# A decoder layer in split float32: weight halves of the memory stage split one unit ahead, squares summed from untransposed rows, output-stage splits at fixed pieces

## The chip, the core and the metric

One core of a Trainium2 chip runs the whole layer. The metric is the device time of one execution in microseconds (us), as the median over several.

## What is computed

One layer of a hybrid decoder for 512 tokens of width 2048, with 256 memory tokens of the same width, all in float32. What the change touches of it:

```python
mem_n = rms_norm(mem, norm_mem_g)
h = rms_norm(x, norm_in_g[layer])
proj = jnp.einsum('bsd,de->bse', h, w_in[layer])
...
mkv = jnp.einsum('bmd,de->bme', mem_n, w_mem_kv[layer])
mk, mv = jnp.split(mkv, 2, axis=-1)
...
merged = (g_a * jnp.einsum('bse,ed->bsd', ya, w_proj_a[layer])
          + g_b * jnp.einsum('bse,ed->bsd', yb, w_proj_b[layer])
          + g_m * jnp.einsum('bse,ed->bsd', ym, w_proj_m[layer]))
x = x + jnp.einsum('bsd,de->bse', merged, w_out[layer])
return rms_norm(x, norm_final_g)
```

`rms_norm` divides each token's row by the root of its mean square and multiplies by a gain. Between the projections and `merged` stand three attention branches, which the change leaves alone.

## The kernel before

**Arithmetic.** Every float32 operand of a large product is split in two parts, hi (the value rounded to TensorE's format, one ACT copy) and lo (value minus hi, one DVE subtraction), and a product is three matmuls: hi·hi, hi·lo, lo·hi. So each weight half of 128x1024 costs one SP transfer of 512 KB, one ACT and one DVE instruction (`load_half`, lines 85 to 92; `parts_1024`, 371 to 376). The split weights live in rings `whi` and `wlo` of three buffers each (WBUFS). `split` (160) does the same for activations.

**Buffers.** Tiles of 128x512 come from 25 buffers (`slot`), those of 128x1024 from 18 (`wide_tile`, shared with the raw weights), tiles of 128x256 from a ring of four (`half_tile`, 368). PSUM has four banks `acc` and four banks `att`.

**Order.** The program is written as one sequence. A planner of the framework orders the instructions of each engine from it: earlier lines have priority, but an instruction whose inputs or buffers are not free by the planner's own durations is passed by later ones. The result is a fixed order for each engine and DMA queue; on the chip each waits at its head.

**Stages.**
1. First projections (275 to 291): three units of w_in, each 2048 x 128, are multiplied by x transposed, in four groups of four k-tiles, while xT comes in. `Rows.cut` (207 to 226) scales and splits each k-tile of xT (216, 217), squares it on ACT (222) and adds the squares up on POOL (226). `Rows.scales` (228) sums over the partitions by one-column matmuls with ones (238), takes the reciprocal root and spreads it over a row (`hrow`) by diagonal matmuls.
2. Three more units of w_in (300 to 310, `project`, 114), 48 matmuls of 512 columns each. Beside them the memory tokens, transposed, are cut in the same way (thi, tlo), and xT is normalized in place (`normalize`, 294).
3. Memory keys (344 to 353): eight units of w_mem, 48 matmuls of 256 columns each. After a unit, DVE multiplies its result by `mrow` (350) and `forms(k)` (317) makes the sums and splits of a pair of k-tiles of h that the later seven-product scheme (Strassen-like, on 256-token halves) needs: four DVE sums, four splits, of which T12 and T3 go to wide tiles.
4. Memory values (354 to 359): two groups of four units, w_mem as the moving operand of 512 columns (`product_rows`, 120), two banks of 128 tokens each. A unit uses both its halves in each bank.
5. The attention branches and gates (to 1084), built on `Pair` (395): two units of w_in in seven products, a generator whose steps are interleaved with attention work. `begin` loads and starts the next pair. Each pair holds half tiles ha, hd and hb between its steps.
6. Output stage (1085 to 1141). The merged activations' parts were written to DRAM (`merged_forms`, 893) and are fetched again as `mg` tiles and split (`left`, `right`, `third_form`, 933 to 945, on `fetch_then`, 907, and `ahead_by`, 918, which fetches some jobs ahead of the split). There are two column pairs of 28 pieces; a piece is one w_out quarter or sum of quarters, split by `prepare` (994) up to two pieces ahead, and 12 matmuls of 512 columns. The seven forms of a pair, four pieces each, are B11, T1, T2, B21, T3, B22, T4, in this order. `multiply` (1006) pops one of the waiting jobs (`later`) after each piece: the right parts at pieces 0 to 7, the third forms at 8 to 15, the T4 parts at 16 to 23.
   After a form, DVE adds its bank to the residual tile (`add_block`, 1029). When a 128x512 block of the result is complete, `gained` (1036) squares it on ACT with a row sum, multiplies it by the final gain on POOL (1039) and, in the first column pair, stores it to DRAM (`rows_done`); the second pair fetches those back. `finish_row` (1043) applies the root of the row's mean square and writes the output. `gf`, the gain spread over the partitions, is loaded at the start of each column pair.

The projection and value loops before, in the lines that matter:

```python
    def project(src, act, tokens=S):
        cut = load_unit(src)
        ps = acc_bank()[:, :tokens]
        product(ps, cut, 0, act, NK)
        return ps
```

`load_unit` loads and splits a half when `product` first asks for it.

## Time and profile before

| | us |
|---|---|
| three timed runs | 2062.39, 2061.36, 2053.85 |
| median | 2061.36 |
| profiled execution | 2054.51 |
| its span, first to last instruction | 2052.7 |
| mean granted TensorE clock | 0.988 of full speed |

PE is TensorE, PEld its weight loads, DVE, ACT and POOL the vector, scalar and GpSimd engines, SP the queue that issues most loads. Times are counted from the start of the span. A wait is named by who waited, the instruction that released it, the us in total, how often and the longest. Matmuls overlap, so the time of one is longer than the step to the next.

### The profile page before, as it was taken

The page shows a single profiled execution, that of the slowest core. Times are in us where ns is not written, and L with a number is a line of the kernel's source. Part 1 is how long each engine was busy: PE and PEld are TensorE (multiplying, and loading weights), DVE is VectorE, ACT ScalarE, POOL GpSimd, SP SyncE. Part 2 cuts the span into 40 slices and gives each one's busy share as a digit, 9 for nine tenths or more (in the row PEclk, how much of TensorE's full clock was granted, in tenths as well). Part 3 has the DMA queues.
Part 4 walks back from the last instruction along what each step waited for, and adds up shares of the span by engine and source line. Part 5 has one row for each costly group of instructions (what it writes and reads, how often), then busy time and mean ns, then how long its engine had stood idle before and what let it go on. Part 6 is the DMA issues. An engine that isn't in the chain of part 4 may idle for free. (4 is left out here: it accounts for less than half of the span.)

```text
span 2052.7 us, 34930 instructions
## 1 busy us (share of the span) xinstructions
PE 1983.7 (97%) x14241; PEld 1870.4 (91%) x14241; DVE 1556.1 (76%) x1940; ACT 1018.8 (50%) x1572; POOL 199.2 (10%) x291
## 2 busy tenths in 40 slices
PE   8868999999999999999999999999999999999898
PEld 5767999889999999889999999998999999998676
DVE  7955777627888888527897979755888888888697
ACT  6624456424666655424646454554444444445445
POOL 4400011010000000001000000001000000012232
PEclk9989999999999999999999999999999999999999
DMA  8226344343332333433332332334434433447664
GB/s 286 88 95 200 129 135 144 129 142 108 98 98 95 101 99 124 149 118 104 103 99 94 104 97 89 114 134 160 157 137 156 138 128 123 156 146 275 213 201 163
DMA packets 88289, 278.52 MB, mean 136 GB/s; under 512 B 16480, under 2 KB 17504, under 8 KB 88128
## 3 DMA queue, kind: packets, MB, share of 16 engines
q1 hardware_dynamic: 70176, 218.72, 32.1%
q0 software_dynamic: 17808, 57.56, 8.2%
q8 instruction: 111, 1.82, 0.4%
q14 instruction: 50, 0.41, 0.1%
q10 hardware_dynamic: 144, 0.02, 0.0%
HBM read 244.76 MB, written 31.49 MB: 135 GB/s over the span
## 5 line engine op out<-in xcount | busy, mean ns | idle before, releaser
L374 ACT ACTIVATE whi<-raw 128x1024 fp32r<-128x1024 f32 x507 | 537.2, 1060 | 611.8 <-PE acc L385 376.9
L375 DVE TENSOR_TENSOR wlo<-raw,whi 128x1024 fp32r<-128x1024 f32 x507 | 622.8, 1229 | 178.3 <-ACT whi L374 167.9
L384 PE MATMUL acc<-kept,whi 128*128 128x256 f32 x2080 | 591.3, 284 | 6.0 <-DVE g L454 5.9
L386 PE MATMUL acc<-kept,wlo 128*128 128x256 f32 x2080 | 588.8, 283 | 0.0
L385 PE MATMUL acc<-kept,whi 128*128 128x256 f32 x2080 | 588.7, 283 | 0.0
L384 PE MATMUL acc<-T,whi 128*128 128x256 f32 x1560 | 442.2, 283 | 0.5 <-ACT ha L430 0.5
L385 PE MATMUL acc<-T,whi 128*128 128x256 f32 x1560 | 441.6, 283 | 0.0
L386 PE MATMUL acc<-T,wlo 128*128 128x256 f32 x1560 | 441.6, 283 | 0.0
L384 PEld LDWEIGHTS acc<-kept,whi 128*128 128x128 f32 x2080 | 399.0, 192 | 7.9 <-issue 7.1
L385 PEld LDWEIGHTS acc<-kept,whi 128*128 128x128 f32 x2080 | 399.1, 192 | 0.3
L386 PEld LDWEIGHTS acc<-kept,wlo 128*128 128x128 f32 x2080 | 399.0, 192 | 0.0
L384 PEld LDWEIGHTS acc<-T,whi 128*128 128x128 f32 x1560 | 299.3, 192 | 1.1 <-ACT ha L430 0.7
L385 PEld LDWEIGHTS acc<-T,whi 128*128 128x128 f32 x1560 | 299.4, 192 | 0.3
L386 PEld LDWEIGHTS acc<-T,wlo 128*128 128x128 f32 x1560 | 299.3, 192 | 0.0
L91 DVE TENSOR_TENSOR wlo<-raw,whi 128x1024 fp32r<-128x1024 f32 x78 | 95.7, 1236 | 149.5 <-ACT whi L90 149.5
L90 ACT ACTIVATE whi<-raw 128x1024 fp32r<-128x1024 f32 x78 | 81.6, 1056 | 167.7 <-PE acc L111 118.1
L110 PE MATMUL acc<-shi,whi 128*128 128x512 f32 x320 | 126.7, 396 | 0.5 <-ACT pr L137 0.5
L111 PE MATMUL acc<-slo,whi 128*128 128x512 f32 x320 | 126.8, 396 | 0.0
L112 PE MATMUL acc<-shi,wlo 128*128 128x512 f32 x320 | 126.0, 394 | 0.0
L423 DVE TENSOR_TENSOR raw<-raw 128x1024 f32<-128x1024 f32 x65 | 79.5, 1223 | 22.4 <-DMA raw<-in_w_in 20.7
L441 DVE TENSOR_TENSOR raw<-raw 128x1024 f32<-128x1024 f32 x65 | 79.4, 1221 | 0.9
L428 DVE TENSOR_TENSOR raw<-raw 128x1024 f32<-128x1024 f32 x65 | 79.3, 1221 | 0.9
(271 smaller groups left out, 2722.0 us busy)
## 6 DMA issues: line engine op xcount, KB each, us to landing
raw<-in_w_in SPq DMA_DIRECT2D x266, 512.0 KB, 3.7
raw<-in_w_out SPq DMA_DIRECT2D x48, 512.0 KB, 5.1
raw<-in_w_mem SPq DMA_DIRECT2D x32, 512.0 KB, 3.7
projected<-pr POOLq DMA_DIRECT2D x48, 256.0 KB, 2.6
pj<-projected POOLq DMA_DIRECT2D x48, 256.0 KB, 4.8
raw<-in_w_pm SPq DMA_DIRECT2D x16, 512.0 KB, 3.8
raw<-in_w_pa SPq DMA_DIRECT2D x16, 512.0 KB, 4.2
xraw<-in_xT SPq DMA_DIRECT2D x16, 256.0 KB, 5.4
```

What stands on the lines that cost most here:

```text
L90: nc.scalar.activation(hi, raw, AF.Copy)
L91: nc.vector.tensor_tensor(lo, raw, hi.bitcast(F32), op=OP.subtract)
L110: nc.tensor.matmul(ps, whi, hi[i], start=i == 0, stop=False)
L111: nc.tensor.matmul(ps, whi, lo[i], start=False, stop=False)
L112: nc.tensor.matmul(ps, wlo, hi[i], start=False, stop=i == n - 1)
L374: nc.scalar.activation(hi, raw, AF.Copy)
L375: nc.vector.tensor_tensor(lo, raw, hi.bitcast(F32), op=OP.subtract)
L384: nc.tensor.matmul(ps, hi[:, sl], f[0], start=start and k == 0, stop=False, skip_group_check=True)
L385: nc.tensor.matmul(ps, hi[:, sl], f[1], start=False, stop=False, skip_group_check=True)
L386: nc.tensor.matmul(ps, lo[:, sl], f[0], start=False, stop=stop and k == 7, skip_group_check=True)
L423: nc.vector.tensor_tensor(s, a21, a22, op=OP.add)
L441: nc.vector.tensor_tensor(s, s, a12, op=OP.add)
```

## The change

- `primed` loads a unit's weights and splits their first half. `project` and `product_rows` take a primed unit, split its second half, and prime the following unit (`follower`) once their matmuls are written, in one chain from the fourth w_in unit through the keys to the last value unit.
- In the memory keys `forms(m - 1)` comes ahead of the multiplication of unit m by mrow. The memory values stand after the definitions of the attention stage, and the first query pair is begun ahead of the last group's copies.
- `Rows.square` loads 128x1024 of x (eight times) or mem (four times) as they are, tokens on partitions, and ACT squares them in place with a sum per token; `scales` adds the two halves' sums on DVE. The transposed squares, the POOL additions and the one-column matmuls go.
- In the output stage a table `beside` says after which piece each split is made: right parts at 4 to 11, third forms two a piece at 12 to 15, T4 parts at 16 to 23, fetched three ahead. The `mg` tiles of 128x256 are half tiles. Squares go to an `att` bank. The gain multiplications move to DVE, after pieces 46 to 51; `rows_done` holds ungained blocks, `gf` is loaded and the blocks are fetched back ahead of B21 of the second column pair. `complete` is what is left of `gained`.

The diff, cut to its core (`M`, `held` and the rest are as before; `finish_row` names `gf[c // 2]` instead of `gf[1]`, and `mem` is a new argument):

```diff
@@ -111,26 +111,34 @@
-    def project(src, act, tokens=S):
+    def primed(src):
         cut = load_unit(src)
+        cut(0, P)
+        return cut
+
+    def project(cut, follower, act, tokens=S):
+
         ps = acc_bank()[:, :tokens]
+        cut(1024, P)
         product(ps, cut, 0, act, NK)
-        return ps
-
-    def product_rows(units, act, tiles, last=1):
+        return ps, primed(follower)
+
+    def product_rows(cut, units, act, tiles):
...
         banks = [acc_bank() for _ in tiles]
-        cuts = [load_unit(u) for u in units]
-        for group in [[u] for u in range(4 - last)] + [list(range(4 - last, 4))]:
+        for u in range(4):
+            now = cut
+            now(1024, P)
+            cut = primed(units[u]) if units[u] is not None else None
             for b, sl in zip(banks, tiles):
-                for k in [4 * u + kk for u in group for kk in range(4)]:
-                    whi, wlo = cuts[k // 4](k % 4 * 512, 512)
+                for k in range(4 * u, 4 * u + 4):
+                    whi, wlo = now(k % 4 * 512, 512)
                     nc.tensor.matmul(b, hi[k][:, sl], whi, start=k == 0, stop=False)
...
                     nc.tensor.matmul(b, lo[k][:, sl], whi, start=False, stop=k == NK - 1)
-        return banks
+        return banks, cut
@@ -188,8 +196,9 @@
-        def __init__(self, cols, w, gain, parts):
-            self.cols, self.w, self.gain, self.parts = cols, w, gain, parts
+        def __init__(self, rows, cols, w, gain, parts):
+            self.rows, self.cols, self.w, self.gain, self.parts = rows, cols, w, gain, parts
+            self.squared, self.sums = 0, sb.tile([P, 2, w // P], F32, name=f"sums{w}")
             self.raw, self.hi, self.lo = [], [], []
@@ -218,26 +227,26 @@
                 self.lo.append(lo[:, sl])
-            sq = slot("sq")
-            nc.scalar.activation(sq, raw, AF.Square)
-            if k0 == 0:
-                self.squares = sq
-            else:
-                nc.gpsimd.tensor_tensor(self.squares, self.squares, sq, op=OP.add)
+
+        def square(self):
+
+            n = self.squared
+            self.squared += 1
+            t = wide_tile("rows")
+            nc.sync.dma_start(t, self.rows[n // 2 * P:(n // 2 + 1) * P, n % 2 * 1024:(n % 2 + 1) * 1024])
+
+            def use():
+                nc.scalar.activation(t, t, AF.Square, accum_out=self.sums[:, n % 2, n // 2:n // 2 + 1])
+            return use
...
             row = slot(name + "row")[:, :self.w]
-            bank = att_bank()
-            per = 512 // self.w
-            for t in range(n):
-                for i in range(per):
-                    c = i * self.w + t * P
-                    nc.tensor.matmul(bank[:, t:t + 1], self.squares[:, c:c + P], ones[:, 0:1], start=i == 0,
-                                     stop=i == per - 1)
-            nc.vector.tensor_copy(col, rstd(bank[:, :n], eps[:, :n]))
+            ss = small([P, n], "ss")
+            nc.vector.tensor_tensor(ss, self.sums[:, 0], self.sums[:, 1], op=OP.add)
+            nc.vector.tensor_copy(col, rstd(ss, eps[:, :n]))
             bank = att_bank()[:, :self.w]
@@ -272,8 +281,13 @@
+    squares = []
     for c in range(4):
         for i, ps in enumerate(first):
+            if 3 * c + i >= 3:
+                squares.append(xrows.square() if len(squares) < 8 else None)
+            if 3 * c + i >= 4:
+                (squares[3 * c + i - 4] or (lambda: None))()
             if c == 3 and i == FIRST - 1:
@@ -295,16 +309,21 @@
-    mrows = Rows(memT, MEM, gains_sb[:, 1, :], lambda k: (slot("thi", F32R), slot("tlo", F32R)))
+    mrows = Rows(mem, memT, MEM, gains_sb[:, 1, :], lambda k: (slot("thi", F32R), slot("tlo", F32R)))
     for c in range(4):
         mrows.load()
+    wcut = primed(w_in[U_ZM + FIRST])
     for i in range(EARLY):
         if i >= FIRST:
-            first.append(project(w_in[U_ZM + i], hT))
+            ps, wcut = project(wcut, w_in[U_ZM + i + 1] if i < EARLY - 1 else w_mem[0], hT)
+            first.append(ps)
+            uses = [mrows.square() for _ in range(2 if i < EARLY - 1 else 0)]
             for c in range(3 if i < EARLY - 1 else 2):
...
                     mrows.load()
+            for use in uses:
+                use()
             for k in range(*((0, 5), (5, 11), (11, NK))[i - FIRST]):
@@ -340,23 +359,17 @@
     mvd = dram.tile([4, P, 512], F32, name="mvd")
-    mrow = None
-    for h in range(4):
-        t = slot("mk")
-        for c in range(2):
-            ps = project(w_mem[2 * h + c], mT, MEM)
-            if mrow is None:
-                mcol, mrow = mrows.scales("m")
-            nc.vector.tensor_tensor(t[:, c * MEM:(c + 1) * MEM], ps, mrow, op=OP.mult)
-            if h or c:
-                forms(2 * h + c - 1)
-        nc.gpsimd.dma_start(mkd[h], t)
-    for g in range(2):
-        banks = product_rows([w_mem[8 + 4 * g + u] for u in range(4)], mT, whole[:2])
-        for t, b in enumerate(banks):
-            nc.gpsimd.dma_start(mvd[2 * g + t], copied(b, "mv", mcol[:, t:t + 1]))
-        if g == 0:
-            forms(7)
+    for m in range(8):
+        if m % 2 == 0:
+            t = slot("mk")
+        ps, wcut = project(wcut, w_mem[m + 1], mT, MEM)
+        if m == 0:
+            mcol, mrow = mrows.scales("m")
+        else:
+            forms(m - 1)
+        nc.vector.tensor_tensor(t[:, m % 2 * MEM:(m % 2 + 1) * MEM], ps, mrow, op=OP.mult)
+        if m % 2:
+            nc.gpsimd.dma_start(mkd[m // 2], t)
     every = slice(None)
@@ -563,6 +576,16 @@
         return parts
+
+    for g in range(2):
+        banks, wcut = product_rows(wcut, [w_mem[8 + 4 * g + u] if 4 * g + u < 8 else None for u in range(1, 5)],
+                                   mT, whole[:2])
+        if g == 0:
+            forms(7)
+        else:
+            pairs_m[0].begin()
+        for t, b in enumerate(banks):
+            nc.gpsimd.dma_start(mvd[2 * g + t], copied(b, "mv", mcol[:, t:t + 1]))
@@ -909,7 +932,7 @@
         def fetch():
-            t = slot("mg")[:, :shape]
+            t = slot("mg") if shape == 512 else half_tile("mg")
             nc.gpsimd.dma_start(t, src)
@@ -1019,8 +1042,8 @@
                     nc.tensor.matmul(banks[t], fl, wh, start=False, stop=last, skip_group_check=True)
-            if later:
-                later.pop(0)()
+            for f in beside.pop(n + i, ()):
+                f()
@@ -1030,15 +1053,17 @@
     def squares_of(t, c):
-        sq = slot("sq")
+        sq = att_bank()
         nc.scalar.activation(sq, rs[t, c], AF.Square, accum_out=parts[:, t, c:c + 1])
-    def gained(t, c):
+    def complete(t, c):
         squares_of(t, c)
-        nc.gpsimd.tensor_tensor(rs[t, c], rs[t, c], gf[c // 2][:, c % 2 * 512:(c % 2 + 1) * 512], op=OP.mult)
         if c < 2:
             nc.gpsimd.dma_start(rows_done[t, c], rs[t, c])
+
+    def gained(t, c):
+        nc.vector.tensor_tensor(rs[t, c], rs[t, c], gf[c // 2][:, c % 2 * 512:(c % 2 + 1) * 512], op=OP.mult)
@@ -1083,13 +1108,14 @@
-    later.extend(ahead_by(2, [right(k) for k in range(8)] + [third_form(k) for k in range(8)]
-                          + [left(k, "T4") for k in range(8)]))
+
+    beside = {}
+    for at, job in zip([4 + k for k in range(8)] + [12 + k // 2 for k in range(8)] + [16 + k for k in range(8)],
+                       ahead_by(3, [right(k) for k in range(8)] + [third_form(k) for k in range(8)]
+                                + [left(k, "T4") for k in range(8)])):
+        beside.setdefault(at, []).append(job)
     for cp in range(2):
         c1, c2, n = 2 * cp, 2 * cp + 1, 28 * cp
-        gf[cp] = wide_tile("gf")
-        nc.sync.dma_start(gf[cp], bass.AP(tensor=gfin.tensor, offset=gfin.offset + 1024 * cp,
-                                          ap=[[0, P], [1, 1024]]))
         xs, ys = [acc_bank() for _ in range(2)], [acc_bank() for _ in range(2)]
@@ -1106,18 +1132,26 @@
             residual(t, c2)
+        if cp:
+            for i in range(2):
+                gf.append(wide_tile("gf"))
+                nc.sync.dma_start(gf[i], bass.AP(tensor=gfin.tensor, offset=gfin.offset + 1024 * i,
+                                                 ap=[[0, P], [1, 1024]]))
+            for t in (2, 3, 0, 1):
+                for c in range(2):
+                    rs[t, c] = fetched(rows_done[t, c], "res")
+            for at, c in ((46, 0), (47, 1), (48, 3)):
+                beside[at] = [lambda c=c: [gained(t, c) for t in (2, 3)]]
+            for at, c in ((49, 0), (50, 1), (51, 2)):
+                beside[at] = [lambda c=c: [gained(t, c) for t in (0, 1)]]
         multiply(zs, n + 12, "B21", True, True)
...
             add_block(t, c1, zs[t], OP.add)
-            gained(t, c1)
-        if cp:
-            for t in (2, 3, 0, 1):
-                for c in range(2):
-                    rs[t, c] = fetched(rows_done[t, c], "res")
+            complete(t, c1)
         multiply(xs, n + 16, "T3", False, False)
...
             add_block(2 + t, c2, xs[t], OP.subtract)
-            gained(2 + t, c2)
+            complete(2 + t, c2)
             if cp:
```

## Rows read from the trace of the kernel before

**Rows 1.** The page, parts 1 and 2: busy time of each engine; TensorE in 40 slices.
```profile
PE 1983.7 (97%) x14241; PEld 1870.4 (91%) x14241; DVE 1556.1 (76%) x1940; ACT 1018.8 (50%) x1572; POOL 199.2 (10%) x291
...
PE   8868999999999999999999999999999999999898
```
**Rows 2.** Windows: us, busy us (count) of PE, PEld, DVE, ACT, POOL, clock, DMA share, GB/s.
```profile
6.30:48.20 41.90, 38.23 (x153) 28.15 (x154) 36.20 (x37) 27.68 (x46) 23.90 (x15) 1.00 0.86 294
48.20:86.80 38.60, 36.03 (x154) 28.80 (x152) 36.51 (x55) 25.11 (x43) 17.64 (x11) 0.96 0.34 119
86.80:166.50 79.70, 57.16 (x398) 54.94 (x397) 48.88 (x89) 29.04 (x44) 6.13 (x6) 0.85 0.32 106
166.50:214.90 48.40, 45.12 (x193) 35.56 (x191) 23.59 (x24) 19.58 (x21) 2.16 (x4) 1.00 0.58 191
214.90:1865.60 1650.70, 1643.69 (x12677) 1593.64 (x12676) 1260.88 (x1551) 829.37 (x1291) 94.40 (x176) 1.00 0.37 124
1865.60:2044.00 178.40, 163.41 (x674) 129.31 (x673) 146.63 (x181) 83.02 (x121) 53.78 (x71) 0.95 0.60 204
2044.00:2052.70 8.70, 0.00 (x0) 0.00 (x0) 2.62 (x8) 2.26 (x5) 0.00 (x0) 0.70 0.62 226
10.00:30.00 20.00, 17.82 (x73) 12.92 (x72) 20.00 (x14) 16.97 (x31) 17.19 (x12) 1.00 0.99 363
```
**Rows 3.** Timeline of PE (start, us): 50 steps of 512 columns, 47 of 256.
```profile
60.12 0.39 PE L111 MATMUL acc<-kept,whi 128*128 128x512 f32 x1
...
71.45 0.39 PE L110 MATMUL acc<-kept,whi 128*128 128x512 f32 x1
...
86.80 0.28 PE L110 MATMUL acc<-thi,whi 128*128 128x256 f32 x1
...
92.34 0.28 PE L112 MATMUL acc<-thi,wlo 128*128 128x256 f32 x1
```
**Rows 4.** Waits of PE over the span: us in total, times, longest.
```profile
PE acc L110 <- ACT whi L90: 19.0, 4, 5.5
PE acc L1019 <- ACT whi L374: 10.5, 4, 4.2
```
**Rows 5.** Timelines of DVE, ACT and PE in the memory keys, of ACT at 1944.
```profile
103.23 2.35 DVE L91 TENSOR_TENSOR wlo<-raw,whi 128x1024 fp32r<-128x1024 f32 x2
111.75 0.42 DVE L350 TENSOR_TENSOR mk<-acc,mrow 128x256 f32<-128x256 f32 x1 [6.17 <-PE acc L112]
...
117.85 3.48 DVE L91 TENSOR_TENSOR wlo<-raw,whi 128x1024 fp32r<-128x1024 f32 x3
...
113.21 0.63 ACT L162 ACTIVATE T<-u 128x512 fp32r<-128x512 f32 x1 [9.54 <-DVE u L323]
...
116.07 2.93 ACT L90 ACTIVATE whi<-raw 128x1024 fp32r<-128x1024 f32 x3
...
117.17 0.58 PE L110 MATMUL acc<-thi,whi 128*128 128x256 f32 x1 [5.45 <-ACT whi L90]
...
1944.42 0.42 ACT L162 ACTIVATE kept<-mg 128x256 fp32r<-128x256 f32 x1 [5.33 <-DMA mg<-waiting]
```
**Rows 6.** Instructions of lines 217 and 226: count, ns shortest/median/longest, first and last start.
```profile
L217 DVE SCALAR_TENSOR_TENSOR kept<-xraw,gains_sb,kept x16: 739/1774/1789, 6.2 to 37.3; 128x512 fp32r<-128x512 f32 x16
...
L226 POOL TENSOR_TENSOR sq<-sq x22: 1327/1618/9679, 7.9 to 89.3; 128x512 f32<-128x512 f32 x22
```
**Rows 7.** Groups by line: count, busy us, mean ns of one, idle before.
```profile
L1079 DVE TENSOR_TENSOR g<-g,g 128x512 f32<-128x512 f32 x32 | 21.9, 685 | 0.0
L1039 POOL TENSOR_TENSOR res<-res,gf 128x512 f32<-128x512 f32 x12 | 21.6, 1809 | 43.3 <-ACT sq L1034 43.3
...
L238 PE MATMUL att<-ones,sq 128*128 128x1 f32 x16 | 1.9, 239 | 0.0
```
**Rows 8.** DMA issues: count, KB each, median us from issue to landing.
```profile
raw<-in_w_out SPq DMA_DIRECT2D x48, 512.0 KB, 5.1
...
mg<-waiting POOLq DMA_DIRECT2D x23, 128.0 KB, 3.0
```

More of the change, by code (lines that the diff above doesn't have):

```diff
@@ L41, in trunk_layer @@
 @with_exitstack
-def trunk_layer(ctx: ExitStack, tc: tile.TileContext, x, xT, memT, gains, gfin, w_in, w_mem, w_pa, w_pb,
+def trunk_layer(ctx: ExitStack, tc: tile.TileContext, x, xT, mem, memT, gains, gfin, w_in, w_mem, w_pa, w_pb,
                 w_pm, w_out, rope, out):
@@ L259, in trunk_layer @@
     kept = [(t[:, 0, :], t[:, 1, :]) for t in held]
-    xrows = Rows(xT, S, gains_sb[:, 0, :], lambda k: kept[k])
+    xrows = Rows(x, xT, S, gains_sb[:, 0, :], lambda k: kept[k])
     hT = xrows.hi, xrows.lo
@@ L958, in trunk_layer @@
     rows_done = dram.tile([4, 2, P, 512], F32, name="rows_done")
-    gf, rs = {}, {}
+    gf, rs = [], {}
     def prepared(c1, c2):
@@ L1050, in finish_row @@
             if c_ == c:
-                nc.vector.scalar_tensor_tensor(y, y, r, gf[1][:, c % 2 * 512:(c % 2 + 1) * 512], op0=OP.mult,
+                nc.vector.scalar_tensor_tensor(y, y, r, gf[c // 2][:, c % 2 * 512:(c % 2 + 1) * 512], op0=OP.mult,
                                                op1=OP.mult)
@@ L1129, in trunk_layer @@
             else:
-                gained(2 + t, c1)
+                complete(2 + t, c1)
         if cp == 0:
@@ L1139, in trunk_layer @@
             else:
-                gained(t, c2)
+                complete(t, c2)
 def _cols(w):
@@ L1188 @@
         "xT": a["x"][0].T.reshape(NK, P, S).transpose(1, 0, 2).reshape(P, NK * S),
+        "mem": a["mem"][0],
         "memT": a["mem"][0].T.reshape(NK, P, MEM).transpose(1, 0, 2).reshape(P, NK * MEM),
```

## The prediction

> **What bounds the kernel now.** The page comes first: TensorE is busy for 97% of the span and its 40 slices show where it is not [rows 1]: in the first four and in the last three. So I cut the span into its stages [rows 2]; the reader is to compare, in each row, the length of the stage with PE's busy time and with the granted clock. The long middle (214.9 to 1865.6 us) has 7 us of idle TensorE in 1650.7: nothing to win there. Everything the change touches lies before and after it.
>
> Busy time hides a slow clock, so I price each stage by the pitch of its matmuls [rows 3]. Fifty steps of 512 columns take 71.45 − 60.12 = 11.33 us, 0.227 each; 47 steps of 256 columns take 5.54 us, 0.118 each, so that a memory-key unit of 48 matmuls is 5.66 us of TensorE. What a stage lasts beyond that is its loss:
> - First projections, 6.3 to 48.2: 144 × 0.227 = 32.6 in 41.9 us; 9.3 lost.
> - Three early units, 48.2 to 86.8: again 32.6, in 38.6 us; 6.0 lost.
> - Memory keys, 86.8 to 166.5: 8 × 5.66 = 45.3 in 79.7 us; 34 lost, at a granted clock of 0.85.
> - Memory values, 166.5 to 214.9: 192 × 0.227 = 43.5 in 48.4 us; 4.9 lost.
> - Output stage, 1865.6 to 2044: 672 × 0.227 = 152.3 in 178.4 us; 26 lost.
>
> What ends the waits: in the memory keys TensorE waits for ACT's first split of a unit, 19 us in 4 waits [rows 4]. The timeline of that stage [rows 5] shows why, and it recurs every two units: DVE makes two splits at 103.2 and then waits 6.2 us for the unit to end, since its next instruction is the multiplication by mrow. Two units' forms fill it until 117.85. Only then come the next splits; ACT, in step, has waited 9.5 us for DVE's u and makes its three splits at 116.07. TensorE idles 5.45 us and restarts at 0.58 us a matmul; the stage's granted clock of 0.85 means that part of it ran at the lower of the two levels, 1.2 GHz. In the output stage it waits for whi too (10.5 us in four waits) [rows 4]; there ACT stands in order behind splits whose input is still on its way from DRAM (5.33 us for one mg at 1944) [rows 5]. In the first stage DVE is busy for the whole of 10 to 30 us [rows 2], and its kept split takes 1.77 us in the median where its shortest takes 0.74, while POOL adds squares [rows 6].
>
> **The change, part by part.** The profiled run took 2054.5 us around a span of 2052.7; the median of the three timed runs, 2061.4, stands 6.9 above it and their lowest 0.7 below it. The sum is made against 2054.5.
>
> *Squares from rows.* Gone: 22 POOL additions, 24 ACT squares of 512, and two groups of eight one-column matmuls (16 in 1.9 us) [rows 7]. Added: 12 ACT squares of 1024 with a sum read out, each about a half split's time (2.93 / 3 us) [rows 5], against twice as many of half the size, so ACT breaks even; one small DVE addition per set; 12 loads of 512 KB on SP's queue, 4 MB of them between 8 and 40 us. Beside it, if the POOL additions are what stretches DVE, the kept splits fall from 1.77 to 0.74 us [rows 6], 16 us over sixteen of them; sixteen at 0.74 and twelve weight splits of 512 columns at about 0.69 [rows 7] are then 20 us of DVE beside TensorE's 32.6, and TensorE sets the pace. I take 3 of the 9.3 us, since 6.3 us of start-up and its slow first matmuls stay. The loads cost nothing while bandwidth is to spare: at 363 GB/s [rows 2] 4 MB are 11.6 us of transfer, and the DMA share of 0.86 leaves 0.14 × 41.9 = 5.9 us. Part of what moves now is prefetch that can come later, so I take no loss; the bounds are −5 (waits and the matmul group gone) and +6 (the whole excess on the path). The 2 MB for the memory rows fall where the share is 0.34 and are free.
>
> The Trainium skill, SBUF — State Buffer, section "SBUF: two separate sides", says that a DVE instruction with two SBUF inputs and a GpSimd instruction that reads SBUF exclude each other for their whole length. The POOL addition of up to 9.7 us agrees. By that rule the 22 additions would give DVE back about 1 us each; the sum by it would be the same 3 us, as TensorE limits the stage then.
>
> *Early units.* The same relief of DVE, and each unit's first half is split while the unit before it runs. 6.0 us lost; I take 3.5 (bounds −5.5 and 0).
>
> *Memory keys.* The next unit's first half is now written ahead of forms and of the mrow multiplication, so the splits no longer stand behind a wait for the unit's end. Forms now come ahead of that multiplication too, so only the second half's split is queued behind its wait. What DVE does per unit is two lower splits (2.35), the multiplication (0.42) and one set of forms ((117.85 − 112.17) / 2 = 2.85): 5.6 us, beside TensorE's 5.66 [rows 5]. So DVE and TensorE come out level, and the 34 us can go almost wholly. The added wait is for the third weight buffer: the half that is split ahead takes it, and the second half of the next unit waits until TensorE is through the first half of this one; it has half a unit, 2.8 us, for a split of 1.1 us on each engine. Two engines filled to the brim and kept in step by in-order queues will not mesh perfectly: I leave 9 us, and take −25. Bounds: −34 and 0 (the planner orders it as before).
>
> *Memory values.* −3 of 4.9: the gap between the two groups, where forms and the copies stood before the first split, is covered by the primed half. Each unit holds both its halves to its end, so the second half of the next is just in time; bounds −4.9 and +1. Starting the first query pair earlier moves nothing: TensorE is full behind it.
>
> *Output stage.* Removed: 12 POOL multiplications of 1.81 us [rows 7], with stores and fetches queued behind them on POOL. Added: 12 DVE multiplications of 0.685 us (as the additions of that form) at pieces 46 to 51, 8.2 us, or 1.37 a piece, beside one split of 1.17 us: 2.5 us against the 2.72 us of twelve matmuls. They fit, barely. The splits of B21 move four pieces later, away from T1's additions, the rest get fixed places and one more fetch ahead; 128 KB fetches come from the ring of four half tiles instead of the 25 slots. In the first column pair DVE stays nearly full: 28 splits and 16 additions at about 1.17 are 51 us, the refetched forms 12 (8 × 0.685 + 16 × 0.42) and twelve block additions 8, 72 us for TensorE's 76, and the front part is denser. So I take 15 of 26 us. Bounds: −23, and +5 if the ring or DVE costs more than the queue gave. The end after the last matmul (8.7 us) is as before: finish_row changes only which gain tile it names.
>
> Sum: −3 − 3.5 − 25 − 3 − 15 = −49.5, so 2005.0 in the profiled run's terms. The timed runs of before lie up to 7.9 us above theirs; as a median I say **2010 us**.
>
> **The rivals.**
> *The planner keeps its pairs (0.14).* The order on each engine comes from a planner that also weighs free buffers and its own durations. If forms of two units still come as one block, the memory keys stay at 79.7: 2010 + 25 = 2035 us. For it: the pattern of two repeats exactly, as tiles shared by two units would make it. Against: the splits now precede forms in the program.
> *DVE takes over the output stage (0.16).* If the dense front of the first column pair sets the pace, 4 us go instead of 15: 2021 us. For it: the 72 us against 76; against: DVE also loses the stretching by POOL's multiplications.
> *The ring of four half tiles (0.06), slower.* 23 small fetches share four buffers, seven of them with the last gate pair's ha, hd and hb, three of which live at once. With one buffer left, each fetch starts after the one before was split, and ACT waits the landing, 3.0 us [rows 8], in order ahead of whi. Uncovered, 23 × 3.0 = 69 us; less the 34.5 of the other stages, with none won here: 2054.5 + 34.5 = 2089 us. It decides the sign from 34.5 / 23 = 1.5 us of uncovered wait per fetch. Against it: in the output stage no gate pair runs.
> [...]
> *The row loads crowd the first weights (0.04).* +6 instead of −3 there: 2019 us.
>
> **How the numbers follow.** The forecast itself has 0.60 and its own range is 1994 to 2026. The range 1994 to 2042 adds the first two rivals with the 7 us spread of the timed runs, and leaves out about 0.15. A measurement of this kernel tells 0.5% (10 us) from no change. Faster by more: the forecast, DVE and row-load cases, and most of the planner case, 0.88; within 0.5%: 0.05; slower: 0.07, the ring and a little more.
>
> **What would show it.** Right: the memory keys last 50 to 58 us at a clock of 0.95 or more, with whi of the next unit ahead of T on ACT; no POOL TENSOR_TENSOR at all; kept splits near 0.74 us; the output stage under 166 us with ACT's waits for mg below 10 us in all. Wrong: three splits in a row on DVE after two sets of forms; ACT waiting for mg between 1840 and 1870; DVE at 10 of 10 through the first column pair with TensorE waiting for wlo; TensorE waiting for xraw's split before 45 us.

## The result, and the profile after

The changed kernel takes 2003.2 us in the median of four runs (2001.22 to 2006.96), the kernel before 2059.39 beside it (2053.85 to 2062.39): a ratio of 0.9732, with a 95% interval of 0.9705 to 0.976. The profiled run is the slowest of the four, 2006.96 us around a span of 2005.2. The forecast was 2010 us, 2005.0 in the terms of the profiled run. So the total came out as said. Its terms did not, and the stages show it. First the page, parts 1 and 2, as in [rows 1]:

```profile
PE 1962.0 (98%) x14225; PEld 1848.9 (92%) x14225; DVE 1530.9 (76%) x1954; ACT 1020.6 (51%) x1573; POOL 135.3 (7%) x257
...
PE   8999999999999999999999999999999999998898
...
POOL 0000010100000000010000000012000000012210
```

The holes in the second to the fourth slice have closed; those at the end stand as they did. The same stages as in [rows 2], cut at the changed kernel's own boundaries (columns as there):

```profile
6.30:43.30 37.00, 37.00 (x152) 29.06 (x152) 22.63 (x42) 28.54 (x47) 0.00 (x0) 1.00 1.02 384
43.30:77.30 34.00, 34.00 (x148) 27.22 (x147) 32.28 (x62) 25.31 (x44) 2.85 (x5) 1.00 0.73 279
77.30:124.70 47.40, 46.18 (x389) 45.49 (x388) 44.26 (x80) 28.54 (x42) 2.17 (x4) 1.00 0.52 177
124.70:169.50 44.80, 44.80 (x195) 36.06 (x193) 24.01 (x24) 20.93 (x22) 2.17 (x4) 1.00 0.61 200
169.50:1818.50 1649.00, 1635.88 (x12678) 1582.96 (x12676) 1256.86 (x1544) 825.91 (x1285) 93.14 (x174) 1.00 0.38 123
1818.50:1995.90 177.40, 163.90 (x674) 128.14 (x672) 147.41 (x199) 86.40 (x128) 33.73 (x62) 0.97 0.59 207
1995.90:2005.20 9.30, 0.19 (x1) 0.00 (x0) 2.69 (x8) 2.26 (x5) 0.00 (x0) 0.76 0.63 228
10.00:30.00 20.00, 20.00 (x86) 16.07 (x85) 10.32 (x17) 16.23 (x27) 0.00 (x0) 1.00 1.02 383
```

Set against [rows 2], the lengths give the account. The boundaries of before are taken here at the first matmul of each stage (86.8, 166.3, 214.9, 1865.6, 2043.7), which moves its rows by 0.3 us at most.

| stage | before, us | after, us | difference | predicted |
|---|---|---|---|---|
| first projections | 42.0 | 37.0 | −5.0 | −3 |
| early units | 38.6 | 34.0 | −4.6 | −3.5 |
| memory keys | 79.5 | 47.4 | −32.1 | −25 |
| memory values | 48.6 | 44.8 | −3.8 | −3 |
| middle | 1650.7 | 1649.0 | −1.7 | 0 |
| output stage | 178.1 | 177.4 | −0.7 | −15 |
| end | 9.0 | 9.3 | +0.3 | 0 |

The memory keys are the gain: 46.18 us of busy TensorE in 47.4, at a granted clock of 1.00 where it was 0.85. The output stage, the second largest term of the forecast, gave nothing. The waits of TensorE over the span (us in total, times, longest), against [rows 4], say where it is still held:

```profile
PE acc L397 <- DVE g L467: 10.9, 8, 3.0
PE acc L1043 <- DVE wlo L388: 9.4, 7, 4.1
...
PE acc L1042 <- ACT whi L387: 4.0, 3, 3.0
PE acc L112 <- DVE wlo L91: 1.1, 2, 0.9
```

The 19.0 us for ACT's first split of a key unit are gone without a successor of any size (1.1 us, L112). In the output stage 10.5 us of waiting for whi and 4.1 for wlo have become 4.0 and 9.4: almost the same sum with the engines exchanged. The row for wlo, from the same view of before:

```profile
PE acc L1020 <- DVE wlo L375: 4.1, 5, 1.7
```

The kept splits, as in [rows 6], fell as the forecast said:

```profile
L226 DVE SCALAR_TENSOR_TENSOR kept<-xraw,gains_sb,kept x16: 742/746/756, 6.3 to 33.4; 128x512 fp32r<-128x512 f32 x16
```

And the small fetches, which landed in 3.0 us in [rows 8] (KB each, median us from issue to landing):

```profile
mg<-waiting POOLq DMA_DIRECT2D x23, 128.0 KB, 5.4
```

### The profile page after: what moved, and what is told of

The parts are those of the page before. It is cut to its first block, busy times and chain, and to the rows that moved or that the text cites. A ratio compares the mean times of both kernels' runs of the same rounds, so it can differ in the third digit from the quotient of the medians.

```text
span 2005.2 us, 34840 instructions
## 1 busy us (share of the span) xinstructions
PE 1962.0 (98%) x14225; PEld 1848.9 (92%) x14225; DVE 1530.9 (76%) x1954; ACT 1020.6 (51%) x1573; POOL 135.3 (7%) x257
## 4 chain that ended last, share of the span: by engine, by line
PE 81%; DVE 6%; DMA 6%; issue 4%; ACT 1%; POOL 1%; ACTq 0%; DVEq 0%; SPq 0%; POOLq 0%
PE acc L397 18%; PE acc L398 18%; PE acc L399 18%; PE acc L112 5%; PE acc L110 5%; PE acc L111 5%; DMA raw<-in_w_in 2%; DVE wlo L388 2%; DMA mg<-waiting 2%; DMA rows_done<-res 1%; PE acc L1043 1%; PE acc L1044 1%; PE acc L1042 1%; ACT whi L387 1%; PE att L162 1%
## 5 line engine op out<-in xcount | busy, mean ns | idle before, releaser
L397 PEld LDWEIGHTS acc<-kept,whi 128*128 128x128 f32 x2080 | 392.8, 189 | 13.7 <-issue 12.8
L398 PEld LDWEIGHTS acc<-kept,whi 128*128 128x128 f32 x2080 | 393.2, 189 | 0.4
L399 PEld LDWEIGHTS acc<-kept,wlo 128*128 128x128 f32 x2080 | 393.2, 189 | 0.0
L112 PE MATMUL acc<-shi,wlo 128*128 128x512 f32 x320 | 126.4, 395 | 0.0
L436 DVE TENSOR_TENSOR raw<-raw 128x1024 f32<-128x1024 f32 x65 | 79.5, 1223 | 25.9 <-DMA raw<-in_w_in 24.2
```

What stands on the lines that cost most here:

```text
L112: nc.tensor.matmul(ps, wlo, hi[i], start=False, stop=i == n - 1)
L397: nc.tensor.matmul(ps, hi[:, sl], f[0], start=start and k == 0, stop=False, skip_group_check=True)
L398: nc.tensor.matmul(ps, hi[:, sl], f[1], start=False, stop=False, skip_group_check=True)
L399: nc.tensor.matmul(ps, lo[:, sl], f[0], start=False, stop=stop and k == 7, skip_group_check=True)
L436: nc.vector.tensor_tensor(s, a21, a22, op=OP.add)
```

## The experiments

Each run but the last was executed once; the kernel before ran beside them at 2058.32 us (e1 to e4), 2057.48 (e5 to e7) and 2061.01 (e8 to e11). Lengths of the stages in us, cut in the same way:

| run | time | first | early | keys | values | middle | output |
|---|---|---|---|---|---|---|---|
| after | 2006.96 | 37.0 | 34.0 | 47.4 | 44.8 | 1649.0 | 177.4 |
| e1, no half ahead | 2015.75 | 37.4 | 34.0 | 54.8 | 45.9 | 1646.9 | 179.4 |
| e2, multiplication first | 2022.54 | 37.1 | 34.0 | 64.1 | 44.8 | 1647.8 | 177.2 |
| e3, old squares | 2021.90 | 42.3 | 34.9 | 58.1 | 44.8 | 1648.7 | 175.9 |
| e4, old output stage | 2006.65 | 37.6 | 34.0 | 47.4 | 44.8 | 1644.5 | 181.1 |
| e5, no ring | 2005.54 | 37.4 | 34.0 | 47.4 | 44.8 | 1645.0 | 179.7 |
| e6, old places | 2007.15 | 37.5 | 34.0 | 47.6 | 44.8 | 1646.9 | 179.3 |
| e7, gain on POOL | 2011.74 | 37.0 | 34.0 | 47.4 | 44.8 | 1650.4 | 180.7 |
| e8, before + order | 2036.13 | 42.0 | 37.0 | 60.3 | 50.9 | 1650.6 | 178.0 |
| e9, before + halves ahead | 2040.95 | 42.0 | 34.1 | 71.7 | 46.0 | 1650.6 | 179.2 |
| e10, half ring | 1993.65 | 37.2 | 34.0 | 47.5 | 44.8 | 1643.3 | 169.6 |
| e11, half ring, late fetch | 1993.40 | 36.9 | 34.0 | 47.4 | 44.8 | 1643.1 | 170.1 |
| e12, e10 again, 5 rounds | 1999.32 | 37.8 | 34.0 | 47.4 | 44.8 | 1649.4 | 170.3 |

(The time of e12 is a median.) e10 and e12 are the same kernel, so they say how far one execution can be trusted: the stages ahead of the middle repeat to 0.6 us, the output stage to 0.7, the middle to 6.1. For the output stage this is too good: e1, e2 and e3 have it as the changed kernel does, and it takes 175.9 to 179.4 us in them, so a difference of some 3 us there says little.

### Memory keys: which edit did it

**e1** loads and splits each half only when its product asks for it, as in the kernel before; nothing is written ahead.

```
     def primed(src):
-        cut = load_unit(src)
-        cut(0, P)
-        return cut
+        return load_unit(src)
...
-        cut(1024, P)
...
-            now(1024, P)
```

> The changed kernel with each half split only when its product asks for it, as before; forms still stand ahead of the multiplication by mrow. If splitting ahead is what shortened the memory keys (47.4 us after, 79.5 before), they are back at 70 to 80 us and the time is near 2030. If the order of forms and multiplication did it, they stay below 52 us and the time near 2006. If POOL's missing additions did it, also below 52 us.

**e2** puts the multiplication by mrow back ahead of the forms.

```
-        else:
-            forms(m - 1)
         nc.vector.tensor_tensor(t[:, m % 2 * MEM:(m % 2 + 1) * MEM], ps, mrow, op=OP.mult)
+        if m:
+            forms(m - 1)
```

> The changed kernel with the multiplication by mrow written ahead of forms again, halves still split ahead. If splitting ahead is the cause, the memory keys stay at 47 to 51 us and the time within 4 us of 2003. If the order of forms and multiplication is the cause, they are back above 65 us and the time above 2020.

**e3** brings back the squares of the transposed pieces: the ACT squares of 512, the POOL additions and the one-column matmuls; the loads of natural rows go.

```
+            sq = slot("sq")
+            nc.scalar.activation(sq, raw, AF.Square)
...
+                nc.gpsimd.tensor_tensor(self.squares, self.squares, sq, op=OP.add)
...
-                squares.append(xrows.square() if len(squares) < 8 else None)
```

> The changed kernel with the squares of the transposed tiles, POOL's additions and the one-column matmuls of before, and without the row loads. If POOL's additions stretch DVE, the first projections are back at 41 to 42 us (37.0 after) and the early units at 36 to 38 (34.0 after), the memory keys stay near 47: about 2011. If the additions cost nothing, both stages stay as after and the time at 2003 or below, the row loads being gone.

The keys measured 54.8, 64.1 and 58.1 us against 47.4: taking the halves away costs 7.4, the order 16.7, the squares 10.7. The three together are 34.8 for a gain of 32.1, so no one edit made it. None of the three fell where a single cause would have put it: 54.8 lies between e1's two cases, 64.1 just under the 65 of e2's second, and e3's keys were to stay near 47. In e2 the windows of the stage show both ways of losing, 11.5 us of idle TensorE and a clock of 0.89, between its levels of 1.2 and 2.4 GHz:

```profile
77.60:141.70 64.10, 52.60 (x389) 51.05 (x388) 46.83 (x82) 29.81 (x44) 2.16 (x4) 0.89 0.39 131
```

Its timelines of DVE and ACT (start, us, instruction, idle time before it and what ended it) show the old knot of [rows 5] on a smaller scale:

```profile
95.50 0.42 DVE L368 TENSOR_TENSOR mk<-acc,mrow 128x256 f32<-128x256 f32 x1 [2.24 <-PE acc L112]
...
101.60 3.48 DVE L91 TENSOR_TENSOR wlo<-raw,whi 128x1024 fp32r<-128x1024 f32 x3
...
96.96 0.63 ACT L170 ACTIVATE T<-u 128x512 fp32r<-128x512 f32 x1 [5.98 <-DVE u L342]
```

DVE stands 2.24 us before the multiplication until the unit has ended, and both sets of forms and three splits are queued behind it; ACT waits 5.98 us for the first u. In the changed kernel the same timelines read:

```profile
92.13 3.48 DVE L91 TENSOR_TENSOR wlo<-raw,whi 128x1024 fp32r<-128x1024 f32 x3
96.27 0.43 DVE L370 TENSOR_TENSOR mk<-acc,mrow 128x256 f32<-128x256 f32 x1 [0.66 <-PE acc L112]
...
97.25 1.23 DVE L91 TENSOR_TENSOR wlo<-raw,whi 128x1024 fp32r<-128x1024 f32 x1 [0.22 <-ACT whi L90]
```

The sign that I had named for being wrong, three splits in a row on DVE behind forms of two units, is there at 92.13. It costs little: the forms ran ahead of the multiplication, while the unit's matmuls ran, and DVE's wait is 0.66 us.

**e8** and **e9** put one of the two edits alone into the kernel before.

e8:
```
-        nc.vector.tensor_tensor(t[:, m % 2 * MEM:(m % 2 + 1) * MEM], ps, mrow, op=OP.mult)
         if m:
             forms(m - 1)
+        nc.vector.tensor_tensor(t[:, m % 2 * MEM:(m % 2 + 1) * MEM], ps, mrow, op=OP.mult)
```

> The kernel before with one edit: in the memory keys forms stand ahead of the multiplication by mrow. Taking that order out of the changed kernel cost its keys 16.7 us, so if the parts add up, the keys fall from 79.5 us by 14 to 20, to 60 to 66 us, and the time to 2036 to 2044. If the order helps only once the halves are split ahead, they stay above 74 us and the time above 2050.

e9 takes `primed`, `project` and `product_rows` from the change and no other part of it:
```
+    def primed(src):
+        cut = load_unit(src)
+        cut(0, P)
+        return cut
```

> The kernel before with the units' first halves split ahead, and nothing else. Taking that out of the changed kernel cost its keys 7.4 us: if the parts add up, the keys fall from 79.5 to 70 to 74 us and the time to about 2050. If splitting ahead is the main cause after all (the prediction's step), they fall below 62 us and the time below 2040.

The keys came to 60.3 us with the order alone (−19.2) and 71.7 with the halves alone (−7.8):

```profile
85.50:145.80 60.30, 50.05 (x397) 48.73 (x397) 48.19 (x90) 28.68 (x43) 7.73 (x6) 0.94 0.38 135
```

```profile
82.70:154.40 71.70, 56.27 (x398) 53.83 (x397) 53.67 (x99) 31.59 (x48) 2.46 (x5) 0.88 0.33 116
```

The first of the two lines is e8's, the second e9's. Of the two the order is the larger whichever way it is measured; the squares alone no run has. e8 gives 2.3 us back in the values (50.9 after 48.6), which its edit does not touch; e9's time fell below the 2050 expected because its early units and values fell too. Beside the order the halves are worth little as long as the old squares stay: e3 has both and takes 58.1 us, 2.2 less than e8. The early units come down to 34 us with the halves alone (e9) or with the new squares and no halves (e1). Most of the gain in the values is one wait between their two groups, in the kernel before (timeline of PE):

```profile
191.60 0.74 PE L130 MATMUL acc<-whi,thi 128*128 128x512 f32 x2 [2.76 <-ACT whi L90]
```

It is gone with the halves alone (e9, 46.0 us) and also with the rest of the change without them (e1, 45.9); on top of that rest the halves are worth 1.1 us.

The squares were expected to act in the first stage. They did: in e3 the stage is back at 42.3 us and the kept splits at 1.77 us in the median, with the POOL additions on beside them.

```profile
L226 DVE SCALAR_TENSOR_TENSOR kept<-xraw,gains_sb,kept x16: 737/1774/1792, 6.4 to 37.5; 128x512 fp32r<-128x512 f32 x16
```

But twice as much, 10.7 us, is lost in the memory keys, where mrow comes late. In e3's timeline DVE still normalizes at 81.87 us, in an instruction stretched to 1.78 us, and copies mrow, which every multiplication of a key unit needs, only at 100.08:

```profile
81.87 1.78 DVE L318 SCALAR_TENSOR_TENSOR xraw<-xraw,gains_sb,hrow 128x512 f32<-128x512 f32 x1
...
100.08 0.42 DVE L267 COPY mrow<-att 128x256 f32<-128x256 f32 x1 [0.64 <-PE att L266]
```

That is 100.08 − 83.6 = 16.5 us into the stage; in the changed kernel it is 85.25 − 77.3 = 8.0. Two things make it late, and no run parts them. DVE arrives behind; and the scale itself has a longer way. In e3 POOL adds the last squares of the memory tokens from 80.06 us, and DVE begins the root (ms) at 95.86 (a line of each timeline):

```profile
80.06 3.04 POOL L236 TENSOR_TENSOR sq<-sq 128x512 f32<-128x512 f32 x2 [0.22 <-ACT sq L232]
```

```profile
95.86 0.14 DVE L184 SCALAR_TENSOR_TENSOR ms<-att,eps 128x2 f32<-128x2 f32 x1
```

In the changed kernel the sums come out of ACT's squares and DVE begins the root ahead of the stage:

```profile
71.64 0.15 DVE L184 SCALAR_TENSOR_TENSOR ms<-ss,eps 128x2 f32<-128x2 f32 x1
...
85.25 0.42 DVE L255 COPY mrow<-att 128x256 f32<-128x256 f32 x1
```

### Output stage: where the 15 us went

**e4** takes the whole output stage from the kernel before (fetches, places, gains on POOL, finish_row).

```
-            t = slot("mg") if shape == 512 else half_tile("mg")
+            t = slot("mg")[:, :shape]
...
-                       ahead_by(3, [right(k) for k in range(8)] + [third_form(k) for k in range(8)]
+                       ahead_by(2, [right(k) for k in range(8)] + [third_form(k) for k in range(8)]
```

> The changed kernel with the output stage of before: jobs popped one a piece from piece 0, mg in slots, gain on POOL, gf early. If the output edits gained 15 us in one place and lost them in another, or did nothing, the stage lasts 177 to 179 us here as in both kernels, and the time is 2003. If the stage of before was helped by something the memory stage's new timing takes away, it is longer than 180 us and the time above 2006.

181.1 us, with 2006.65 in all, inside the range of the changed kernel's own runs: the stage's edits together are worth 3.7 us there, and nothing that one execution can tell in the total. The same stage took 178.1, 178.0 and 179.2 us in the kernel before, e8 and e9, so some 2 to 3 of the 3.7 us belong to the new timing ahead of it or to scatter.

**e5** takes all fetches from the 25 slots, with the rest of the change kept.

```
-            t = slot("mg") if shape == 512 else half_tile("mg")
+            t = slot("mg")[:, :shape]
```

> The changed kernel with the small mg fetches in the 25 slots instead of the ring of four half tiles. If the ring is what holds them back, ACT's waits for mg (30 us in 17 waits after) fall below 15 us, TensorE's waits at 1771 and 1822 us (3.0 and 4.1) go, and the span falls by 5 to 12 us. If the ring costs nothing, the output stage stays at 176 to 179 us and the span within 2 us of 2005.

**e6** puts the splits back at their old pieces, one fetch less ahead.

```
-    for at, job in zip([4 + k for k in range(8)] + [12 + k // 2 for k in range(8)] + [16 + k for k in range(8)],
-                       ahead_by(3, [right(k) for k in range(8)] + [third_form(k) for k in range(8)]
+    for at, job in zip(list(range(24)),
+                       ahead_by(2, [right(k) for k in range(8)] + [third_form(k) for k in range(8)]
```

> The changed kernel with the splits of the output stage at their places of before (right parts at pieces 0 to 7, third forms at 8 to 15, T4 parts at 16 to 23, two fetched ahead). If the fixed places are worth what the ring takes back, the output stage is longer by 4 us or more than the 177.4 after. If the planner moves them anyway, it stays within 2 us.

**e7** puts the gains back on POOL.

```
-        nc.vector.tensor_tensor(rs[t, c], rs[t, c], gf[c // 2][:, c % 2 * 512:(c % 2 + 1) * 512], op=OP.mult)
+        nc.gpsimd.tensor_tensor(rs[t, c], rs[t, c], gf[c // 2][:, c % 2 * 512:(c % 2 + 1) * 512], op=OP.mult)
```

> The changed kernel with the gain multiplications on POOL, in their new place. DVE's one wait of 6.7 us for the blocks fetched back, and TensorE's 2.3 us behind it at 1925, should go; if POOL's multiplications stretch DVE, that comes back as up to 12 x 1 us of DVE time late in the stage, where DVE has room. The moved gains as a cost: span lower by 2 to 4 us. As a gain: higher by 2 or more.

With the gains on POOL the stage takes 180.7 us against 177.4, and waits for wlo come up late in it, the longest 2.4 us; with the old places it takes 179.3. So the gains on DVE are worth some 3 us and the places 2, neither clear of what the stage varies by without an edit. e5 shows where the ring acts, since it exchanges one wait for another and the span falls by 1.4 us only. In the changed kernel POOL's timeline (DMA issues) shows the seven fetches for B11 beside the last gate pair:

```profile
1796.82 0.55 POOL L936 DMA_DIRECT2D mg<-waiting  x1 [32.69 <-DVE g L473]
1811.09 0.56 POOL L936 DMA_DIRECT2D mg<-waiting  x1 [13.72 <-issue]
...
1814.83 0.55 POOL L936 DMA_DIRECT2D mg<-waiting  x1 [1.26 <-DVE g L467]
1818.41 0.55 POOL L936 DMA_DIRECT2D mg<-waiting  x1 [3.04 <-DMA mg<-waiting]
```

One fetch has gone out before 1811 us; the rest follow one by one, three of them behind an instruction of DVE that frees a half tile, as the first did. What held the second for 13.72 us the profile does not name. Meanwhile DMA is full of the output stage's first weights (windows as above):

```profile
1798.00:1806.00 8.00, 8.00 (x69) 8.00 (x68) 7.70 (x10) 4.09 (x6) 0.00 (x0) 1.00 0.24 89
1806.00:1826.00 20.00, 15.94 (x120) 14.73 (x118) 10.93 (x16) 8.83 (x15) 3.30 (x6) 1.00 1.01 380
```

So the late fetches also land slowly, in 5.3 us in the median of these seven, and ACT and DVE stand in order behind them (timelines of the two):

```profile
1817.24 0.42 ACT L170 ACTIVATE kept<-mg 128x256 fp32r<-128x256 f32 x1 [3.29 <-DMA mg<-waiting]
...
1823.77 0.42 ACT L170 ACTIVATE kept<-mg 128x256 fp32r<-128x256 f32 x1 [2.88 <-DMA mg<-waiting]
1824.09 1.04 ACT L387 ACTIVATE whi<-raw 128x1024 fp32r<-128x1024 f32 x1
...
1825.16 1.22 DVE L388 TENSOR_TENSOR wlo<-raw,whi 128x1024 fp32r<-128x1024 f32 x1
```

TensorE waits 4.1 us for that wlo, the longest wait of the stage. In e5 it is gone and fetches land in 3.1 us, but the later forms' fetches now come from the same slots as the rows and the wide fetches, and TensorE stands at T3 instead, behind ACT, which waits there for mg (DMA issues; waits of PE over the stage, us in total, times, longest):

```profile
mg<-waiting POOLq DMA_DIRECT2D x23, 128.0 KB, 3.1
```

```profile
PE acc L1042 <- ACT whi L387: 8.9, 2, 8.5
```

Hence **e10**, in which the B11 fetches come from slots and the later ones from the ring:

```
-    def fetch_then(src, shape, use):
+    def fetch_then(src, shape, use, ring=True):
...
-            t = slot("mg") if shape == 512 else half_tile("mg")
+            t = half_tile("mg") if shape == 256 and ring else slot("mg")[:, :shape]
...
-        return fetch_then(waiting[k][:, c], 256, lambda t: split(t, M[form][k]))
+        return fetch_then(waiting[k][:, c], 256, lambda t: split(t, M[form][k]), form != "B11")
```

> The changed kernel with the seven B11 fetches, which run beside the last gate pair, in the 25 slots, and the sixteen third-form and T4 fetches still in the ring of four. If the ring hurts only where ha, hd and hb share it, TensorE's wait of 4.1 us at the second piece goes, the wait of 8.5 us that all-slots brought at T3 does not come, and the span is 1999 to 2003 against 2005.2. If slots and ring are worth the same, it stays at 2003.5 to 2007.

**e11** is e10 with the fetch of the parked rows (the `rows_done` loop) moved behind B21. It is aimed at one more wait of the changed kernel, where DVE reaches a gain multiplication whose rows are not back:

```profile
1925.77 0.69 DVE L1066 TENSOR_TENSOR res<-res,gf 128x512 f32<-128x512 f32 x1 [6.68 <-DMA res<-rows_done]
```

> The same with the stored blocks fetched back after B21 of the second column pair, as before, instead of ahead of it. If the early fetch lures the planner into placing a gain multiplication where DVE then waits 6.7 us for it, that wait and TensorE's 2.3 us at 1925 go and the span is 1 to 3 us below that of the hybrid. If the slots decide when the fetch runs, it is within 1 us of it.

e11 changed nothing: the eight fetches are issued at the times of e10 to 0.3 us (the first at 1910.1 after 1910.3, the others from 1929.7 after 1929.9), the wait is still 6.0 us and the time 1993.40 against 1993.65. Where the fetch stands in the program doesn't decide it; that a free slot does is argued, not shown. **e12** times e10's kernel.

> The kernel of e10 timed in rounds beside the kernel before. If the 1993.7 us of its one run stands, the ratio is 0.966 to 0.971, its interval below 0.9732, the changed kernel's. If that run was a lucky one of the same kernel, the ratio is 0.971 to 0.975.

It takes 1999.32 us (1998.94 to 2000.86, five runs), 0.9714 of the kernel before (0.9699 to 0.9729). By what was expected the ratio lies just on the side of the lucky run: of e10's lead only the output stage's part stands, 170.3 us after 169.6, where the middle is back at 1649.4. But e10 and e11 ran on one chip, with spans of 1991.9 and 1991.6 us, and the five runs of e12 on another, with 1997.2 to 1999.1: the lead may belong to the chip and not to luck, which no run tells. The waits of TensorE in the stage (e12, rows as above) are what e10 was to bring, without the 4.1 us for wlo and the 8.5 at T3:

```profile
PE acc L1042 <- ACT whi L387: 4.6, 3, 3.0
PE acc L1043 <- DVE wlo L388: 4.0, 4, 1.9
```

POOL's timeline of e12 shows how it is won; six of the seven fetches are out before 1804 us, ahead of the stretch in which DMA is full:

```profile
1766.38 0.55 POOL L936 DMA_DIRECT2D mg<-waiting  x1 [0.29 <-issue]
1779.51 0.56 POOL L936 DMA_DIRECT2D mg<-waiting  x1 [12.58 <-DVE g L1102]
...
1803.88 0.55 POOL L936 DMA_DIRECT2D mg<-waiting  x1 [1.50 <-ACT ha L443]
1807.59 0.55 POOL L936 DMA_DIRECT2D mg<-waiting  x1 [3.15 <-issue]
```

```profile
1806.00:1826.00 20.00, 19.17 (x136) 17.52 (x134) 15.83 (x26) 9.81 (x17) 1.77 (x4) 1.00 0.97 373
```

```profile
1819.90:1990.30 170.40, 161.67 (x674) 127.12 (x672) 143.93 (x193) 82.66 (x122) 32.17 (x59) 0.98 0.60 210
```

TensorE is busy for 19.17 of those 20 us, where it was 15.94. The second of the two lines is the whole stage. The half ring beats the kernel before; that it beats the changed kernel is likely (its slowest run lies below the other's fastest) and small, 0.2%, and the two intervals overlap.

## Why the prediction was right in its total and wrong in its parts

- **Squares: right, and too small.** The step from POOL's additions to the kept splits held to the number (0.74 forecast, 0.746 measured), no POOL addition is left, and TensorE waited for no transfer: it is busy for all of 37.0 us at a DMA share of 1.02. The Trainium skill, SBUF — State Buffer, section "SBUF: two separate sides", says that a DVE instruction with two SBUF inputs and a GpSimd instruction that reads SBUF shut each other out; the trace agrees in both directions: the kept splits fall from 1774 to 746 ns and are back at 1774 in e3. I took 3 us, 5.0 came; e3 gives them back. What the forecast left out is the second place. It followed the relief of DVE up to the early units and stopped; the 10.7 us that e3 loses in the memory keys had no term, neither for DVE's backlog nor for a scale that is ready earlier.
- **Early units and values: right in size**, −4.6 for −3.5 and −3.8 for −3. For the early units either of the two means I named is enough (e1, e9). For the values I named the gap between the groups and the primed half. The gap was there, 2.76 us, and the half alone closes it (−2.6 in e9); but the rest of the change closes it too, so that the half adds 1.1 us of the 3.8 (e1).
- **Memory keys: right mechanism, one part missing, wrong weights and size.** The failed step is the 9 us left for engines that "will not mesh perfectly". Against 45.3 us of matmuls 2.1 were lost. And the forecast put the split ahead first and named the order of forms and multiplication second; the runs put them the other way, 19.2 to 7.8 alone and 16.7 to 7.4 taken out. The part of the squares, 10.7 taken out, it did not have.
- **The planner's pairs: half true.** The pairs are still there and the stage doesn't care: what cost time was the wait in front of them (2.24 us at 95.50 in e2, 0.66 at 96.27 in the changed kernel), not the block. The sign by which I would have known that I was wrong was badly chosen.
- **Output stage: wrong, −0.7 for −15.** The failed step is the sentence against the ring, that "in the output stage no gate pair runs". The rival had named seven fetches that share the ring with the last gate pair, and that sentence set them aside. These seven, for B11, are issued from 22 us ahead of the stage to 2.5 us into it, beside the last gate pair, and there the mechanism of the slower rival acts: a fetch goes out only when a half tile has come free. With their buffers alone exchanged (e10, e11, e12) the stage falls to 170. The ring acted on seven fetches, not 23, so the price was some 7 us and not 69: 177.4 less 169.6 and 170.3. The landing, too, was not the 3.0 us of [rows 8] but 5.3, as the fetches fell into a full DMA. Even without this the term was too large, 8 us and not 15, and no run shows why. The half ring's stage still holds 18 us over the 152.3 of its matmuls: 8.7 of idle TensorE, of which one wait for whi of 3.0, and the rest busy time beyond the pitch, at a granted clock of 0.98.
- **DVE as the bound: not seen.** DVE is busy for 147.41 of 177.4 us and took the gain multiplications without a loss; on POOL they made the stage 3 us longer (e7). The Trainium skill, SBUF — State Buffer, section "SBUF: two separate sides", warns in its box on the "DVE blocks DMA" trap that GpSimd cannot write the descriptors of the DMAs it issues while DVE runs an instruction in a 2-port performance mode (as a float32 copy within SBUF does), and says that `tensor_tensor`, the form of the splits and of the gain multiplications, has no such mode. The trace agrees: in e5 the small fetches land in 3.1 us with DVE busy for 144 of 179.7.
- **From the profiled run to the median: wrong by some 9 us.** The profiled run of before was among its fastest, so I raised 2005.0 to 2010. The profiled run of after was the slowest of its four, 3.8 above the median. One execution says little about where in the scatter it lies. Two misses of opposite sign, 14 us too much in the output stage and 11 too little ahead of the middle, made the total look better than its parts: that it came so close is luck.

Open: what moves the middle between 1643 and 1649 us. From 1402 us on the changed kernel's TensorE waits seven times for DVE's g (L467), about every 61 us, up to 3.0 us at 1771. These waits sum to 10.6 us there and to 10.8 in e12, where the middle takes 1649 us, but to 6.5 in e10, the same kernel as e12, and 6.6 in e4, where it takes 1643 and 1645: some 4 of the 6 us. No run tried the fetch of pj that stands beside them.

## What to carry to other kernels

An instruction that waits for the end of a unit holds all that is queued behind it on its engine: put work that doesn't need the wait ahead of it before you move work to other engines. Where a stage's engine is filled, follow its backlog, and each value that the next stage waits for, into that stage, because a relief may pay there more than where it is made. Before a small ring takes over fetches, list all that uses it at the moment they are issued, and look at DMA's share in the stretch where they would land; here a mixture of two buffer sources did better than either.

## What was not expected of the hardware

- Idle TensorE is paid for twice here. Over the 45.3 us of key matmuls the busy time grows with the idle time in six kernels: idle 1.2 and busy 46.2 (after), 6.3 and 48.5 (e1), 10.3 and 50.1 (e8), 11.5 and 52.6 (e2), 15.4 and 56.3 (e9), 22.5 and 57.2 (before, [rows 2]), with the granted clock falling from 1.00 over 0.97, 0.94, 0.89 and 0.88 to 0.85. It is no fixed rate: e3 is idle for 6.0 us only, and busy for 52.1 at a clock of 0.91.
- A DMA share of 1.02 at 384 GB/s over the whole first stage, 0.86 before, cost TensorE not one wait there; I had allowed for up to 6 us.
- The 128 KB fetches land in 3.0 us in [rows 8] and in 5.3 where 512 KB weight loads fill DMA beside them (share 1.01). Those take 11.2 us themselves in the median between 1795 and 1830 us, and 6.5 over the whole run.
